# A list scheduler that keeps TensorE on plain fp32 work before it returns to fp32r products

## The chip, the cores and the metric

The kernel runs on one core of a Trainium2 chip. The time is device microseconds of one execution of the whole program on that core, from launch to end; of several runs the median is given. A core has TensorE (PE; its weight loads are a queue of their own, PEld), VectorE (DVE), ScalarE (ACT), GpSimd (POOL) and SyncE (SP), which here only issues DMAs. Each engine works through its own list of instructions in order and waits for the other engines by semaphores.

## The reference

One step of a streaming encoder layer, for a prompt of 512 rows and a sample of 64 rows (576 rows in all, model width 1024). It is all fp32.

```python
h = rms_normalize(x) * g_norm_mix * (1.0 + sc1) + sh1
q, k, v, qi, ki, wi, z, xbc, dt, gate_logits = jnp.split(h @ w_in, offs, axis=-1)
q = rope(rms_normalize(q) * g_q, pos); k = rope(rms_normalize(k) * g_k, pos)
qi = rope(qi, pos); ki = rope(ki, pos)
# branch A: an indexer scores every key, each query keeps the top 128 or 256, softmax over those
logits = jnp.einsum('thd,sd->ths', qi, ki_all); score = sum_h wi * relu(logits)
_, idx = lax.top_k(score, topk); o_attn = softmax(q . k_all[idx]) @ v_all[idx]
# branch B: causal convolution of width 4, Mamba-2 scan in chunks of 64, gated group norm
y, h_last = ssd_scan(silu(causal_conv(xbc)), dt, -exp(a_log), bm, cm, state_ssm)
y = rms_normalize((y + d_skip * xh) * silu(z)) * g_ssm_norm
mixed = (g_attn * (o_attn @ w_branch_attn) + g_ssm * (y @ w_branch_ssm)) @ w_out
x = x + gt1 * mixed
h2 = rms_normalize(x) * g_norm_ffn * (1.0 + sc2) + sh2
gate, up = jnp.split(h2 @ w_gate_up, 2, axis=-1)
x = x + gt2 * ((silu(gate) * up) @ w_down)
```

(Shapes are left out and some lines are drawn together.) Outputs are x of both groups and the new keys, values, indexer keys, convolution rows and SSD states.

## The kernel before

**Three kinds of TensorE work.** Every large product is made of three fp32r products: weights and activations are split into a high part that fp32r holds exactly and a rest (`wh`, `wl`; `hTh`, `hTl` for the activations), and `hTh·wh + hTl·wh + hTh·wl` is summed in PSUM. The split of each weight tile (512 KB, from `raw`) is made by ScalarE (`wh`) and VectorE (`wl`). These are 8,776 of the 10,078 matmuls. What has to be exact, or is small, is plain fp32: 681 transposes against the identity (`ident`) and 94 plain products (the indexer's `kis·qis`, the states' `xw·bt` and others); the profile has two records for each plain product. The third kind, 527 products, are plain fp32 on column tiles: they give `tile_position`, use 32 or 64 columns of the array only, and several of them share it.

**Stages.** Up to about 47 us the modulation vectors and the first norm; to 240 us the projections of q, k, v and of the indexer, and the selection of keys; to 480 us attention over four key heads (`key_stack`, `q_stack`, `softmax_rows`, `pv`, `make_q`), between which `fillers` puts columns of the input projection that are not needed yet (fp32r); to 786 us the convolution and the scan (`conv`, `chunk`, `stage_a`, `stage_b`, `stage_c`), with the rest of the input projection beside it; to 976 us the products of the two branches and of the output; then the feed-forward part, to 1364 us.

**What sets the order.** No instruction is issued where it is written. `Plan` (l.248) records each as an `Op` with its engine, its dependences and a duration from a table (`cost`, l.341). `order` (l.391 to 508) then plays the whole program through by these durations: at each step it takes the engine that is free first, moves what has become ready by then into that engine's heap, and takes the op with the lowest priority number (`op.prio`, the place in which it was written, less an offset that stages give themselves). `emit` (l.511) writes the instructions out in that sequence, so nearly every row of the profile bears the one line 533 (535 with the change), and rows are told apart by the names of their tiles. On the chip each engine keeps the order that the plan found, whatever the real durations are.

**The rule for TensorE** (l.457 to 471). `_columns_of_tile` (l.226) gives an op the width of its column tile, or 0. While the last op taken was on a column tile (`tile_cols` not 0), ops of the same width that are ready go first, even where another has the lower number; and where the width changes, the plan's clock is put forward by 0.095 us. Plain fp32 work and fp32r products both have 0, and between them the priority alone decides. Matmuls of TensorE carry a slack of 0.25 us on their inputs in the plan (`SLACK`).

**Names at the places spoken of.** `tok` are rows from the token-major part that are transposed into `py`/`px` (the PSUM tiles; `mm` is the third pool of PSUM tiles, of the large products). `lg` are the indexer's logits, brought out of PSUM by ScalarE after the products `kis·qis`. In the scan, `ssum`/`sq`·`pick` are column-tile products into `px`, which VectorE copies to `rowsZ`, which TensorE transposes (`px<-ident,rowsZ`); `cu` are steps of the convolution on VectorE (l.1324 on), `xdt` and `xw` scaled inputs of the scan, `xw·bt` the product of the states. `kd` are cached keys, which are transposed for attention.

Of the kernel before, what the change touches and what calls it, by code (L numbers as in the profile page):

```python
# [6 lines left out]
F32R = mybir.dt.float32r  # L7
# [217 lines left out]

def _columns_of_tile(op):

    return op.args[0].shape[0] if op.kw.get("tile_position") is not None else 0


def _cols(v):
# [16 lines left out]
class Plan:  # L248
# [142 lines left out]
    def order(self):  # L391
# [16 lines left out]
        seq, dma_free, queue, now_ev, port, tile_cols = [], 0.0, 0.0, 0, 0.0, 0  # L408

        def enable(op):  # L410
            closed = [p for p in op.pools if not p.open]
            if closed:
                held.setdefault(closed[0], []).append(op)
                return
            t = 0.0
            for d, kind in op.deps.items():
                q = ops[d]
                if q.mm and op.mm:
                    t = max(t, q.t0)
                elif kind == "raw" or q.eng != op.eng:  # L420
                    t = max(t, q.t1 + self.LATENCY[q.eng][op.eng] + op.slack)
            heapq.heappush(future[op.eng], (t, op.prio, op.i))

        def fire():
            nonlocal now_ev
            while now_ev < len(self.events):
                what, p = self.events[now_ev]
                if what == "close" and p.ops_left:
                    return
                seq.append((what, p))  # L430
                now_ev += 1
                if what == "open":
                    p.open = True
                    for op in held.pop(p, []):
                        enable(op)
# [6 lines left out]
        while n < len(ops):  # L442
            best, at = None, None
            for e in engs:
                if ready[e]:
                    t = free[e]
                elif future[e]:
                    t = max(free[e], future[e][0][0])
                else:
                    continue  # L450
                if at is None or t < at:
                    best, at = e, t
            assert best is not None, ("stuck", n, len(ops), self.events[now_ev:now_ev + 1])
            f, r = future[best], ready[best]
            while f and f[0][0] <= at:
                t, pr, i = heapq.heappop(f)
                heapq.heappush(r, (pr, i))
            pr, i = heapq.heappop(r)
            op = ops[i]
            if best == "tensor":  # L460
                if tile_cols and _columns_of_tile(op) != tile_cols:
                    same = [x for x in r if _columns_of_tile(ops[x[1]]) == tile_cols]
                    if same:
                        heapq.heappush(r, (pr, i))
                        pr, i = min(same)
                        r.remove((pr, i))
                        heapq.heapify(r)
                        op = ops[i]
                if _columns_of_tile(op) != tile_cols:
                    at += 0.095  # L470
                tile_cols = _columns_of_tile(op)
            if op.port:
                if port > at and best == "vector":
                    held_back = [(pr, i)]
                    while r and op.port and len(held_back) < 6:
                        pr, i = heapq.heappop(r)
                        held_back.append((pr, i))
                        op = ops[i]
                    pr, i = held_back.pop() if not op.port else held_back.pop(0)
                    op = ops[i]  # L480
                    for x in held_back:
                        heapq.heappush(r, x)
                if op.port:
                    at = max(at, port)
                    port = at + op.dur
            op.t0 = at
            if best == "sync":
                queue = max(at, queue) + 0.46
                dma_free = max(queue + 1.3, dma_free) + op.bytes / 360e3
                op.t1 = dma_free + op.dur_dma  # L490
            elif op.fn == "dma_start":
                dma_free = max(at + op.dur + 1.0, dma_free) + op.bytes / 185e3
                op.t1 = dma_free + op.dur_dma
            else:
                op.t1 = at + op.dur
            free[best] = max(at + op.dur, dma_free - 2.0 if best == "sync" else 0.0)
            seq.append(op)
            n += 1
            for p in op.pools:
                p.ops_left -= 1  # L500
            for s in op.succ:
                ops[s].left -= 1
                if ops[s].left == 0:
                    enable(ops[s])
            fire()
# [35 lines left out]
def build(tc, I, O):  # L541
# [1466 lines left out]
    def prepare_more():  # L2008
        with R.prio(4000):
            more = True  # L2010
            while more:
                more = False
                n = sum(1 for o in slices if o not in rawd and (o in wd or o == ("pair", 0, 0) and ("pair", 0, 1) in wd))
                while loaded[0] < len(slices) and loaded[0] < n + NRAW:
                    load_slice()
                    more = True
                if made[0] < len(order):
                    more = prepare_down() or more
# [106 lines left out]
```

## Time and profile before

| what | value |
|---|---|
| median of 3 runs | 1367.02 us (1366.27 to 1367.84) |
| the profiled execution's own time | 1366.41 us |
| its span, first to last instruction | 1364.4 us |
| mean granted TensorE clock | 0.998 |
| ScalarE busy, whole span | 54% |
| GpSimd busy, whole span | 18% |
| DMA | 199.52 MB, 146 GB/s on average |
| TensorE in the chain that ended last | 89% of the span |

The span is the profiled execution from its first to its last instruction; its own time has 2.0 us more around it. Busy time of TensorE is the union of the matmuls, whose ends are modelled; weight loads (PEld) lie beside them. Rows of the timeline give a start and a duration in us, then the instruction, as output tile, arrow, input tiles; a number behind an x says how many alike follow one another. What stands in brackets is idle time of the engine ahead of the row and what ended it.

### The profile page before, as it was taken

Reading aid. Unit: us, or ns where it says so; the run is one execution under the profiler, and the core shown is the slowest. Engines: PE = TensorE matmul, PEld = TensorE weight load, DVE = VectorE, ACT = ScalarE, POOL = GpSimd, SP = SyncE. Lnnn points to the kernel's source line nnn. Section 1 sums busy time; section 2 is a strip of 40 time slices with the busy share of each in tenths; the row PEclk is TensorE's granted clock in tenths of the full one; section 3 lists DMA queues with packets and bytes.
Section 4 is the critical chain, followed back from the end, with each engine's and each line's share of the span. In section 5 each row is a group of like instructions: output and inputs, shape, how many; then the busy total and the mean of one; then the engine's idle time right before and its main releaser. Section 6 shows DMA issues by size and latency. Waiting matters only on the chain.

```text
span 1364.4 us, 27749 instructions
## 1 busy us (share of the span) xinstructions
PE 1346.8 (99%) x10699; PEld 1311.9 (96%) x10699; DVE 1106.6 (81%) x2237; ACT 733.0 (54%) x1535; POOL 240.2 (18%) x370
## 2 busy tenths in 40 slices
PE   7999999999999999999999999999999999999998
PEld 5999999999999999999999999999999999999998
DVE  5689998887778788888887599857899998878564
ACT  5445343776776766666675342225566665665221
POOL 1312002230310235545453200001000000000000
PEclk9999999999999999999999999999999999999999
DMA  9762435675754454454536698748233343325431
GB/s 298 227 178 84 109 104 140 142 164 126 179 140 116 137 168 118 117 153 122 150 96 193 209 316 241 224 147 257 73 109 94 109 124 94 93 77 156 123 107 36
DMA packets 267332, 199.52 MB, mean 146 GB/s; under 512 B 25152, under 2 KB 239328, under 8 KB 267200
## 3 DMA queue, kind: packets, MB, share of 16 engines
q1 hardware_dynamic: 263248, 183.59, 46.1%
q0 software_dynamic: 3952, 14.16, 5.2%
q8 instruction: 84, 1.38, 0.4%
q14 instruction: 48, 0.39, 0.1%
HBM read 157.75 MB, written 28.96 MB: 137 GB/s over the span
## 4 chain that ended last, share of the span: by engine, by line
PE 89%; DVE 6%; DMA 2%; issue 1%; SPq 1%; ACT 1%; POOL 0%; ACTq 0%; DVEq 0%; POOLq 0%
PE mm L533 64%; PE py L533 14%; PE px L533 11%; DVE score L533 1%; DMA raw<-in_w_in 1%; DVE m L533 1%; DVE wl L533 1%; SPq L533 1%; DMA xt<-in_x_sample 1%; DVE y L533 0%; DVE xlS L533 0%; DMA rawu<-in_w_gate_up 0%; DVE wh L533 0%; DVE tok L533 0%; DVE f L533 0%
## 5 line engine op out<-in xcount | busy, mean ns | idle before, releaser
L533 ACT ACTIVATE wh<-raw 128x1024 fp32r<-128x1024 f32 (+3 forms) x152 | 149.3, 984 | 209.0 <-PE mm L533 149.5
L533 PE MATMUL mm<-hTl,wh 128*128 128x288 f32 (+1 forms) x1024 | 231.9, 302 | 0.0
L533 PE MATMUL mm<-hTh,wh 128*128 128x288 f32 (+1 forms) x1024 | 231.7, 303 | 0.0
L533 PE MATMUL mm<-hTh,wl 128*128 128x288 f32 (+1 forms) x1024 | 230.7, 302 | 0.5 <-DVE wl L533 0.5
L533 PEld LDWEIGHTS mm<-hTh,wh 128*128 128x128 f32 (+1 forms) x1024 | 165.7, 189 | 3.6 <-issue 1.3
L533 PEld LDWEIGHTS mm<-hTl,wh 128*128 128x128 f32 (+1 forms) x1024 | 167.0, 189 | 1.8 <-issue 0.9
L533 PEld LDWEIGHTS mm<-hTh,wl 128*128 128x128 f32 (+1 forms) x1024 | 165.6, 189 | 2.5 <-issue 1.1
L533 DVE TENSOR_TENSOR wl<-raw,wh 128x1024 fp32r<-128x1024 f32 (+2 forms) x109 | 131.3, 1205 | 30.7 <-ACT wh L533 26.3
L533 DVE SCALAR_TENSOR_TENSOR cu<-xc,wc,cu 128x579 f32<-128x579 f32 x96 | 83.4, 869 | 2.0 <-ACT cu L533 1.0
L533 PE MATMUL mm<-wh,hTh 128*128 128x256 f32 x256 | 72.4, 285 | 0.0
L533 PE MATMUL mm<-wh,hTl 128*128 128x256 f32 x256 | 72.2, 284 | 0.0
L533 PE MATMUL mm<-wl,hTh 128*128 128x256 f32 x256 | 71.9, 282 | 0.0
L533 DVE SCALAR_TENSOR_TENSOR aacc<-adr,sil,aacc 128x512 f32<-128x512 f32 x84 | 58.7, 749 | 5.3 <-DMA adr<-in_w_ada 5.2
L533 PE MATMUL mm<-yh,wl 128*128 128x288 f32 x256 | 55.2, 296 | 0.0
L533 PE MATMUL mm<-yh,wh 128*128 128x288 f32 x256 | 55.0, 296 | 0.0
L533 PE MATMUL mm<-yl,wh 128*128 128x288 f32 x256 | 54.9, 296 | 0.0
L533 PE MATMUL mm<-xhS,wh 128*128 128x290 f32 (+1 forms) x248 | 54.8, 296 | 0.0
L533 ACT ACTIVATE P<-lg,mn 128x128 f32<-128x128 f32 (+4 forms) x72 | 41.7, 581 | 19.6 <-DVE mn L533 18.8
L533 PE MATMUL mm<-xhS,wl 128*128 128x290 f32 (+1 forms) x232 | 51.3, 296 | 0.0
L533 ACT ACTIVATE dec<-dec,nacs 128x128 f32<-128x128 f32 x128 | 42.4, 393 | 14.8 <-POOL dec L533 14.8
L533 PEld LDWEIGHTS mm<-wh,hTh 128*128 128x128 f32 x256 | 48.0, 188 | 0.5 <-issue 0.4
L533 PEld LDWEIGHTS mm<-wh,hTl 128*128 128x128 f32 x256 | 48.2, 189 | 0.2
(518 smaller groups left out, 3955.5 us busy)
## 6 DMA issues: line engine op xcount, KB each, us to landing
raw<-in_w_in SPq DMA_DIRECT2D x80, 512.0 KB, 4.3
adr<-in_w_ada SPq DMA_DIRECT2D x36, 512.0 KB, 4.8
raw<-in_w_gate_up SPq DMA_DIRECT2D x22, 512.0 KB, 3.9
wl<-raw POOLq DMA_DIRECT2D x21, 512.0 KB, 5.2
rawu<-in_w_gate_up SPq DMA_DIRECT2D x20, 512.0 KB, 4.0
bc<-acs_d SPq DMA_DIRECT2D x32, 256.0 KB, 3.4
raw<-in_w_branch_ssm SPq DMA_DIRECT2D x16, 512.0 KB, 4.5
raw<-in_w_down SPq DMA_DIRECT2D x16, 448.0 KB, 3.9
```

The costliest lines, as they stand in the source:

```text
L533: getattr(engines[x.eng], x.fn)(*[real(a) for a in x.args], **{k: real(v) for k, v in x.kw.items()})
```

## The change

`_columns_of_tile` now knows three kinds: the width for column tiles, 0 for fp32r products, and -1 for everything else, which is plain fp32 products and all transposes. Since -1 counts as true, the rule "while the last op was of a kind other than 0, ready ops of the same kind go first" now holds for plain fp32 work too: TensorE stays on it while any is ready, and then takes what has the lowest number. From fp32r it leaves as before, as soon as an op of another kind has the lowest number. The second hunk gives a change between plain fp32 and fp32r a price of 0.03 us in the plan; changes to or from a column tile keep 0.095.

```diff
 def _columns_of_tile(op):
 
-    return op.args[0].shape[0] if op.kw.get("tile_position") is not None else 0
+    if op.kw.get("tile_position") is not None:
+        return op.args[0].shape[0]
+    return 0 if op.fn == "matmul" and op.args[2].dtype == F32R else -1
...
                 if _columns_of_tile(op) != tile_cols:
-                    at += 0.095
+                    at += 0.095 if max(_columns_of_tile(op), tile_cols) > 0 else 0.03
                 tile_cols = _columns_of_tile(op)
```

The instructions are the same ones. Their order differs from about 47 us (TensorE's 295th matmul) to 976 us, and behind 790 us only here and there: in 3,762 of TensorE's positions, 642 of VectorE's 2,173, 437 of ScalarE's 1,460, 98 of GpSimd's 375 and 72 of SyncE's 509. Most moves are of a few positions, up to about 50; four transposes of `kd` go from a group at 214 us to 107 us. Groups of plain fp32 work between fp32r products were 263 and are 239; changes between the two kinds were 504 and are 455. The 52 groups on column tiles have the same sizes.

The first place is at about 97 us, TensorE, in the projection of the sample's rows. Before:

```order
L533 MATMUL mm_114<-wl_106,hsS_128 128x256
L533 MATMUL mm_114<-wh_101,hsS_128 128x256
L533 MATMUL mm_114<-wl_104,hsS_128 128x256
L533 MATMUL py_110<-ident_70,tok_651 128x128
L533 MATMUL px_113<-ident_70,tok_651 128x128 x4
L533 MATMUL mm_114<-wh_101,hsS_128 128x256
```

With the change:

```order
L535 MATMUL mm_114<-wl_106,hsS_128 128x256
L535 MATMUL mm_114<-wh_101,hsS_128 128x256
L535 MATMUL py_110<-ident_70,tok_650 128x128
L535 MATMUL px_113<-ident_70,tok_650 128x128 x4
L535 MATMUL mm_114<-wl_104,hsS_128 128x256
L535 MATMUL mm_114<-wh_101,hsS_128 128x256
```

The five transposes of `tok` stand one fp32r product earlier.

The second place is at about 176 us, TensorE, where the indexer's products (`kis·qis`, plain fp32) stand among fp32r products. Before:

```order
L533 MATMUL mm_114<-hTl_127,wh_101 128x288 x2
L533 MATMUL py_110<-kis_670,qis_671 128x384 x2
L533 MATMUL mm_114<-hTh_126,wl_104 128x288 x2
L533 MATMUL mm_114<-hTh_126,wh_101 128x288 x2
L533 MATMUL py_111<-kis_670,qis_671 128x384 x2
```

With the change:

```order
L535 MATMUL mm_114<-hTl_127,wh_101 128x288 x2
L535 MATMUL mm_114<-hTh_126,wl_104 128x288 x2
L535 MATMUL mm_114<-hTh_126,wh_101 128x288 x2
L535 MATMUL py_110<-kis_669,qis_670 128x384 x2
L535 MATMUL mm_114<-hTl_127,wh_101 128x288 x2
L535 MATMUL mm_114<-hTh_126,wl_104 128x288 x2
L535 MATMUL py_111<-kis_669,qis_670 128x384 x2
```

The first index product stands four fp32r products later, the second two.

The third place is at about 568 us, in the scan, behind a group on column tiles. On TensorE, before:

```order
L533 MATMUL px_112<-sq_5063,pick_120 32x64
L533 MATMUL mm_114<-hTh_126,wh_103 128x288 x2
L533 MATMUL mm_114<-hTl_127,wh_103 128x288 x2
L533 MATMUL mm_114<-hTh_126,wl_106 128x288 x2
L533 MATMUL mm_114<-hTh_126,wh_103 128x288 x2
L533 MATMUL mm_114<-hTl_127,wh_103 128x288 x2
L533 MATMUL mm_114<-hTh_126,wl_106 128x288 x2
L533 MATMUL py_111<-xw_5048,bt_5050 128x256
L533 MATMUL mm_114<-hTh_126,wh_103 128x288 x2
L533 MATMUL mm_114<-hTl_127,wh_103 128x288 x2
L533 MATMUL px_113<-ident_70,rowsZ_5034 128x128 x2
```

With the change:

```order
L535 MATMUL px_112<-sq_5040,pick_120 32x64
L535 MATMUL mm_115<-hTh_126,wh_101 128x288
L535 MATMUL mm_115<-hTl_127,wh_101 128x288 x2
L535 MATMUL mm_115<-hTh_126,wl_104 128x288 x2
L535 MATMUL mm_115<-hTh_126,wh_101 128x288
L535 MATMUL py_111<-xw_5025,bt_5027 128x256
L535 MATMUL mm_115<-hTh_126,wh_101 128x288
L535 MATMUL mm_115<-hTl_127,wh_101 128x288 x2
L535 MATMUL px_113<-ident_70,rowsZ_5011 128x128 x2
```

Between the group and the transposes of `rowsZ` stood 16 fp32r products and one plain product, and now stand nine and the same one. On VectorE at that place, before:

```order
L533 TENSOR_TENSOR wl_105<-raw_99,wh_102 128x1024
L533 SCALAR_TENSOR_TENSOR cu_5077<-xc_5075,wc_78,cu_5077 128x579
L533 TENSOR_TENSOR xdt_5046<-px_113,dtp_88 128x256
L533 SCALAR_TENSOR_TENSOR cu_5077<-xc_5075,wc_78,cu_5077 128x579
L533 TENSOR_TENSOR xw_5048<-px_113,wst_90 128x256
L533 SCALAR_TENSOR_TENSOR cu_5077<-xc_5075,wc_78,cu_5077 128x579
L533 COPY rowsZ_5034<-px_112 128x128
```

With the change:

```order
L535 TENSOR_TENSOR xdt_5023<-px_113,dtp_88 128x256
L535 TENSOR_TENSOR xw_5025<-px_113,wst_90 128x256
L535 TENSOR_TENSOR wl_106<-raw_100,wh_103 128x1024
L535 COPY rowsZ_5011<-px_112 128x128
L535 COPY rowsZ_5011<-px_112 32x64
L535 SCALAR_TENSOR_TENSOR cu_5053<-xc_5051,wc_78,cu_5053 128x579
```

The three steps `cu` that stood ahead of the copy and among `xdt` and `xw` stand behind it or elsewhere, and `wl` stands directly ahead of it.

## The prediction

> **What bounds the kernel now.** I began with the page's first two parts, busy time by engine and the 40 slices, to see whether one engine is the limit everywhere.
>
> ```profile
> PE 1346.8 (99%) x10699; PEld 1311.9 (96%) x10699; DVE 1106.6 (81%) x2237; ACT 733.0 (54%) x1535; POOL 240.2 (18%) x370
> PE   7999999999999999999999999999999999999998
> ```
>
> TensorE is busy in 99% of the span and in every slice but the first and the last. A change to its order can therefore gain in two ways only: its instructions take less time in the new order, or its idle time goes. To see where idle time is left I cut the span at the places where the order of the change begins to differ (47 us) and ends to differ (976 us), and once more at 786 us, behind which the two orders are nearly the same.
>
> ```profile
> 0.00:47.00 47.00, 37.73 (x424) 30.18 (x424) 21.82 (x55) 22.55 (x40) 7.32 (x22) 0.96 0.98 294
> 47.00:786.00 739.00, 736.75 (x5919) 714.09 (x5919) 616.09 (x1313) 435.90 (x955) 223.89 (x329) 1.00 0.53 142
> 786.00:976.00 190.00, 190.00 (x1494) 187.45 (x1492) 151.75 (x259) 66.57 (x121) 8.99 (x20) 1.00 0.72 225
> 976.00:1364.40 388.40, 382.33 (x2869) 380.21 (x2867) 316.97 (x612) 207.93 (x420) 0.00 (x0) 1.00 0.34 98
> ```
>
> The second row is the stage that the change reorders (projections, attention, SSD): 739.00 us, of which TensorE is busy in 736.75, so 2.25 us are idle. The idle 15 us of the first and last rows lie where the change moves nothing. Busy PE hides small waits, since the ends of matmuls are modelled. So I also read the waits of the weight loads, which come one ahead of each matmul, in that same stage (waited for, us in total, times, longest).
>
> ```profile
> PEld py L533 <- issue: 4.7, 26, 0.3
> PEld mm L533 <- issue: 2.5, 14, 0.2
> PEld px L533 <- issue: 1.0, 5, 0.3
> PEld py L533 <- DVE tok L533: 1.0, 1, 1.0
> PEld py L533 <- ACT vst L533: 0.9, 1, 0.9
> PEld py L533 <- ACT lg L533: 0.8, 2, 0.6
> PEld px L533 <- POOL dec L533: 0.5, 3, 0.2
> PEld px L533 <- ACT dec L533: 0.5, 3, 0.2
> PEld py L533 <- DVE qst L533: 0.3, 1, 0.3
> PEld px L533 <- DVE qis L533: 0.2, 1, 0.2
> PEld py L533 <- DVE rowsZ L533: 0.2, 1, 0.2
> PEld px L533 <- DVE kst L533: 0.2, 1, 0.2
> ```
>
> The nine rows that name an engine add up to 4.6 us in 14 waits. The three "issue" rows (8.2 us in 45 gaps) wait for nothing that the profile shows; I find them mostly where TensorE goes to or from column tiles. That is all the waiting there is to win in 739 us.
>
> **The change part by part.** It takes no instruction away and adds none: 10,078 matmuls in both orders, and the same work on the other engines. It moves 3,762 positions on TensorE, mostly by fewer than 50. Groups of plain fp32 work between fp32r products fall from 263 to 239, so there are 24 groups fewer; the 52 groups on column tiles keep their number and sizes. The first question is what a group costs beyond its instructions. The timeline of TensorE (start, duration, instruction, count) has a group of one transpose and a group of eight:
>
> ```profile
> 781.74 0.43 PE L533 MATMUL mm<-oh,wh 128*128 128x288 f32 x2
> 782.01 0.29 PE L533 MATMUL mm<-ol,wh 128*128 128x288 f32 x1
> 782.14 0.27 PE L533 MATMUL px<-ident,cvo 128*96 128x128 f32 x1
> 782.17 0.38 PE L533 MATMUL mm<-ol,wh 128*128 128x288 f32 x1
> 782.39 0.42 PE L533 MATMUL mm<-oh,wl 128*128 128x288 f32 x2
> ```
>
> ```profile
> 214.31 0.43 PE L533 MATMUL mm<-hTh,wl 128*128 128x288 f32 x2
> 214.58 1.03 PE L533 MATMUL px<-ident,kd 128*128 128x128 f32 x8
> 215.37 0.51 PE L533 MATMUL mm<-hTh,wh 128*128 128x288 f32 x2
> 215.72 0.43 PE L533 MATMUL mm<-hTl,wh 128*128 128x288 f32 x2
> ```
>
> Starts are to be read here, since durations overlap. Two fp32r products take 0.27 us (781.74 to 782.01), so 0.133 each. From 781.74 to 782.39 is 0.65 us with four of them (0.53), which leaves 0.12 for a group of one transpose. From 214.31 to 215.72 is 1.41 us with four products again, which leaves 0.88 for eight transposes, 0.11 each. If a group cost something to enter or to leave, the one transpose would show all of it: 0.12 less 0.11 is **0.01 us a group**. Terms of the sum:
>
> - 24 groups fewer at 0.01: **-0.24 us**. Bounds: 0, and 0.06 for each (the starts are printed to 0.01 us, and the 0.12 is a difference of several), -1.5 in all.
> - The four transposes of cached keys that go from about 214 us to about 107 us stand amid fp32r products in both places: 0, and their cover is the same work.
>
> The second question is which waits change, since merging moves work past the products that covered its wait. Three places carry the rest. The first is the start of the stage, in the weight loads:
>
> ```profile
> 96.40 0.19 PEld L533 LDWEIGHTS mm<-wl,hsS 128*128 128x128 f32 x1
> 97.57 0.14 PEld L533 LDWEIGHTS py<-ident,tok 128*128 128x128 f32 x1 [0.98 <-DVE tok L533]
> ```
>
> The transposes of tok wait 0.98 us for VectorE. They now stand one product earlier, and a product of 256 columns takes at most the 0.133 us of one with 288; the wait ends when VectorE is done, as before, and the product now runs behind it: **+0.1 us**. Everything behind the transposes on TensorE waits with them. Bounds 0 (if VectorE comes earlier by as much) and +0.13.
>
> The second place is the index product at 175.9 us, which waits for ScalarE's logits to leave PSUM:
>
> ```profile
> 175.16 0.43 PE L533 MATMUL mm<-hTl,wh 128*128 128x288 f32 x2
> 175.92 0.63 PE L533 MATMUL py<-kis,qis 128*128 128x384 f32 x2 [0.33 <-ACT lg L533]
> ```
>
> Two products from 175.16 end at 175.43 by the price above, and the index product starts at 175.92: 0.49 us lost. In the new order four more fp32r products (0.53 us) stand ahead of it and cover all of that: **-0.5 us**. Bounds 0 (ScalarE's evictions, themselves behind an index product, come later by as much) and -0.6, the longest wait of the row "ACT lg". What is late next is the following index product, which keeps its distance of three to four products.
>
> The third place stands for the SSD stage, where three such groups follow a column-tile group:
>
> ```profile
> 567.96 0.43 PE L533 MATMUL mm<-hTh,wl 128*128 128x288 f32 x2
> 568.32 0.45 PE L533 MATMUL px<-ssum,pick 128*32 128x128 f32 x8
> ...
> 568.89 0.28 PE L533 MATMUL px<-sq,pick 128*32 128x64 f32 x2
> 569.10 0.54 PE L533 MATMUL mm<-hTh,wh 128*128 128x288 f32 x2
> ...
> 571.77 0.38 PE L533 MATMUL px<-ident,rowsZ 128*128 128x128 f32 x2
> ```
>
> and VectorE beside it:
>
> ```profile
> 570.32 0.81 DVE L533 SCALAR_TENSOR_TENSOR cu<-xc,wc,cu 128x579 f32<-128x579 f32 x1
> 571.05 0.40 DVE L533 COPY rowsZ<-px 128x128 f32<-128x128 f32 x2
> ```
>
> VectorE's copy of rowsZ ends at 571.45, and its transposes start at 571.77, so 0.32 us are to spare. In the new order seven fp32r products fewer stand ahead of the transposes (7 x 0.133 = 0.93). With the copy as late as before, the transposes would wait 0.93 less 0.32, 0.6 us, at each of three places: +1.8. But VectorE's order changes as well: the convolution steps (cu, 0.81 us each) that stood between ready work and the copy are now two fewer, 1.6 us, which is more than the 0.6. I take **0**, bounds 0 and +1.8, since the new order shows both moves. Before the last wait of attention (ACT vst, 0.9 us) 20 products stand in both orders, so nothing changes there.
>
> The planner also charges 0.03 us at each of 455 switches, which moves other engines' work against TensorE; that is in the order already, and costs nothing by itself.
>
> Sum on the profiled execution (its own time 1366.41, with a span of 1364.4): 1366.41 - 0.24 + 0.1 - 0.5 + 0 = 1365.8. That execution is 0.6 us under the median of the runs (1367.02), so 1366.4 for the median.
>
> **The rivals.**
>
> Faster: merging groups covers most named waits. If all nine rows went, 1366.41 - 0.24 - 4.6 = 1361.6, or 1362.2 for the median. For it: a rule that makes bigger groups leaves longer stretches of fp32r products between them, as at 175.9 us. Against it: of the 4.6 us I find 0.5 that goes; the first two waits (1.9 us) stand behind work that keeps its cover or loses some.
>
> Faster by a price for the switch: entering a column-tile group costs 0.09 us (568.32 less the end of two products from 567.96, 568.23), and leaving about 0.10 (two records of some 0.055 from 568.89 end at 569.00, the next product starts at 569.10). If TensorE paid as much between plain fp32 and fp32r, 24 groups x 0.19 = 4.6 us would go: 1366.41 - 4.6 + 0.1 - 0.5 = 1361.4, or 1362.0. Against it stand the 0.01 us of the single transpose. The Trainium skill's page "TensorEngine Tiling (Array Packing)", section "Key Properties", says that TensorE drains when the tiling mode changes, and not when only the tile does. By that rule a price belongs at the column-tile groups alone, where the trace agrees with 0.19 us; the single transpose at 782.14 shows none.
>
> Slower: merged groups run before their input is ready. A group is prolonged with work that became ready only in the plan; on the chip its producer is late, TensorE works in order, and all fp32r products queued behind it wait too. The price at one place is 0.6 us at worst (rowsZ), and 0.33 us on the mean of the 14 waits (4.6 / 14). It decides the sign from 3.3 us on (2.7 for 0.2%, and the 0.6 gained above): six places at 0.6, or ten at 0.33. If half of the 24 merged groups wait 0.33, it is +4.0: 1369.8, or 1370.4 for the median. For it: the stage has only 2.25 us of idle time, so new waits have no slack to fall into. Against it: groups merge mostly by holding back fp32r products that were ready, and VectorE is busy for 616 of 739 us, ahead of TensorE nearly everywhere.
>
> That the change does nothing is told apart from these by the order: it does merge, though only 24 groups of 263.
>
> **How the numbers follow.** A measurement of this kernel can tell about 0.2% (2.7 us) from no change. The forecast has 0.69; its own range is 1364.9 (all of the -1.5 and -0.6) to 1368.9 (no gain, rowsZ at +1.8 and tok at +0.1). Faster by covered waits gets 0.14, faster by a price of the switch 0.03, slower by late inputs 0.14. The range reaches to 1362.0 and to 1370.4, which leaves out the tails of both sides, and takes in the bounds of each term. Faster 0.17, same 0.69, slower 0.14.
>
> **What would show it.** In the stage 47 to 786 us TensorE's busy time and the length should change by under 2 us. A group of one transpose should still add 0.12 us. The wait for tok should be about 1.1 us, the one for ACT lg at 175.9 us gone, and no wait for rowsZ above 0.2. If groups of equal size take less time than before, the price of the switch is the wrong step. If new rows for VectorE or ScalarE above 0.5 us stand among the waits, it is the cover. A change behind 976 us, where the order is the same, would be no work of this change.

## The result: 0.6% slower, by waits in the attention and scan stages

| | median, us | range | runs |
|---|---|---|---|
| before | 1367.12 | 1366.27 to 1367.84 | 6 |
| with the change | 1375.15 | 1373.79 to 1376.10 | 6 |

The ratio is 1.0058, 95% interval 1.0048 to 1.0069: 8.0 us slower, outside the range that was given (1362.0 to 1370.4). The profiled execution took 1373.79 us, its span 1372.0 us, 7.6 more than before. Of e14, an experiment below, one run is left out of the median: it took 2178.55 us at a granted clock of 0.557.

These are the windows of the changed kernel, cut where the same work begins and ends (us; busy time and count of PE, PEld, DVE, ACT, POOL; clock; DMA share; GB/s):

```profile
0.00:47.00 47.00, 37.23 (x425) 29.71 (x425) 22.12 (x56) 22.80 (x41) 7.64 (x24) 1.00 0.98 295
47.00:794.50 747.50, 740.04 (x5918) 714.60 (x5919) 622.92 (x1312) 435.61 (x955) 233.63 (x327) 1.00 0.52 140
794.50:984.50 190.00, 190.00 (x1493) 187.38 (x1492) 151.79 (x259) 66.62 (x121) 9.00 (x20) 1.00 0.72 225
984.50:1372.00 387.50, 381.98 (x2869) 380.06 (x2868) 316.94 (x612) 208.42 (x420) 0.00 (x0) 1.00 0.34 99
```

The second stage holds all of the loss: 747.5 us for what took 739.0, with as many matmuls (5,918 for 5,919). Up to TensorE's 2,500th record, at 317 us, only 0.4 us of it has come; nearly all of it lies in attention and the scan. The third stage takes the same 190.0, the fourth 0.9 less. TensorE's weight loads are busy for 714.60 us as before (714.09), so TensorE's instructions became no dearer. (The matmuls' busy time is 3.3 us more, but their ends are modelled.) What grew is the waiting of those loads in that stage (engine and line, waited for, us in total, times, longest):

```profile
PEld py L535 <- issue: 4.7, 21, 1.4
PEld py L535 <- ACT decS L535: 3.2, 2, 1.8
PEld mm L535 <- issue: 2.5, 14, 0.2
PEld py L535 <- ACT lg L535: 1.3, 2, 1.1
PEld px L535 <- issue: 0.8, 5, 0.2
PEld py L535 <- ACT qst L535: 0.8, 1, 0.8
PEld px L535 <- DVE dec L535: 0.7, 1, 0.7
PEld py L535 <- DVE qst L535: 0.6, 2, 0.3
PEld px L535 <- DVE xb L535: 0.6, 1, 0.6
PEld py L535 <- DVE tok L535: 0.6, 1, 0.6
...
PEld py L535 <- DVE rowsZ L535: 0.2, 1, 0.2
```

The rows of this view that name an engine or a DMA add up to 13.2 us in 33 waits; before they were 4.6 us in 14. An "issue" row holds a 1.4 us wait that is none of the column tiles' small ones; it is the one at 510 us below. With the three "issue" rows (8.0 us, before 8.2) the view adds up to 21.2 us, before to 12.8. The difference, 8.4 us, accounts for the 8.5 by which the stage is longer.

**Three long waits, all for the states' product xw·bt.** The longest, at 743 us, seen on TensorE, ScalarE, GpSimd and VectorE:

```profile
741.09 0.29 PE L535 MATMUL mm<-hTh,wh 128*128 128x288 f32 x1
743.00 0.67 PE L535 MATMUL py<-xw,bt 128*128 128x256 f32 x2 [1.61 <-DVE xw L535]
```

```profile
740.80 0.35 ACT L535 ACTIVATE decS<-decS,nacs 64x64 f32<-64x64 f32 x1 [1.59 <-POOL decS L535]
741.06 0.85 ACT L535 ACTIVATE cu<-xc,bconv,wc 128x579 f32<-128x579 f32 x1
741.82 0.25 ACT L535 ACTIVATE bt<-px 128x128 f32<-128x128 f32 x1
```

```profile
740.36 0.41 POOL L535 TENSOR_SCALAR_AFFINE_SELECT decS<-bc 64x256 f32<-64x256 f32 x1 [4.70 <-DMA bc<-acs_d]
```

```profile
742.10 0.42 DVE L535 TENSOR_TENSOR xdt<-px,dtp 128x256 f32<-128x256 f32 x1 [2.26 <-ACT bt L535]
742.44 0.41 DVE L535 TENSOR_TENSOR xw<-px,wst 128x256 f32<-128x256 f32 x1
```

Read backwards: TensorE waits for xw, VectorE waits for ScalarE's bt, and bt stands, one convolution step between, behind an exponential of decS that waits for GpSimd, which waits for a DMA. (The waits of the loads above put this wait down to decS at once.) Nothing in bt needs decS; it is only next in line. The same happens at 592.7 us.

That neighbour is not new. Before, all four of these exponentials stood ahead of the same bt, and nothing was lost:

```profile
729.70 1.07 ACT L533 ACTIVATE decS<-decS,nacs 64x64 f32<-64x64 f32 x4 [1.24 <-POOL decS L533]
730.99 0.27 ACT L533 ACTIVATE bt<-px 128x128 f32<-128x128 f32 x1
```

```profile
730.67 0.27 PE L533 MATMUL px<-ident,bcx 128*128 128x128 f32 x1
732.78 0.59 PE L533 MATMUL py<-xw,bt 128*128 128x256 f32 x2
```

There the transpose that bt copies out of PSUM (`px<-ident,bcx`) came 0.97 us behind the first exponential, which therefore held up nothing. In the changed kernel the same transpose is at 739.38, 1.42 us ahead of the exponential. The new order used up what there was to spare between TensorE and the DMA that feeds decS.

At 510.2 us xw·bt waits for its PSUM tile, which VectorE's xb steps free:

```profile
507.90 1.77 DVE L535 SCALAR_TENSOR_TENSOR cu<-xc,wc,cu 128x579 f32<-128x579 f32 x1
509.60 0.46 DVE L535 SCALAR_TENSOR_TENSOR xb<-xb,dcol,py 128x64 f32<-128x64 f32 x2
```

```profile
508.74 0.29 PE L535 MATMUL mm<-hTh,wh 128*128 128x288 f32 x1
510.20 0.67 PE L535 MATMUL py<-xw,bt 128*128 128x256 f32 x2 [1.16 <-DVE xb L535]
```

At 510, 593 and 743 us xw·bt starts 1.46, 1.49 and 1.91 us after the fp32r product ahead of it, which takes 0.13. Lost are 1.33 + 1.36 + 1.78 = 4.5 us, over half of the 8. Before, the same three products started 0.13 us after the one ahead, without a wait.

### The profile page after: what moved, and what is told of

It reads as the page before. It is cut to its first block, busy times and chain, and to the rows that moved or that the text cites. A ratio compares the mean times of both kernels' runs of the same rounds, so it can differ in the third digit from the quotient of the medians.

```text
span 1372.0 us, 27773 instructions
## 1 busy us (share of the span) xinstructions
PE 1349.2 (98%) x10699; PEld 1311.8 (96%) x10699; DVE 1113.8 (81%) x2237; ACT 733.4 (53%) x1535; POOL 250.3 (18%) x370
## 4 chain that ended last, share of the span: by engine, by line
PE 76%; DVE 8%; issue 2%; DMA 2%; ACT 2%; POOL 1%; SPq 0%; ACTq 0%; POOLq 0%; DVEq 0%
PE mm L535 54%; PE py L535 13%; PE px L535 10%; DVE wl L535 1%; DVE score L535 1%; DVE m L535 1%; DVE f L535 1%; DMA bc<-acs_d 1%; DMA o_d<-oT 1%; DVE T L535 1%; DVE cu L535 0%; DVE wh L535 0%; ACT wh L535 0%; DMA rawu<-in_w_gate_up 0%; DVE gg L535 0%
## 5 line engine op out<-in xcount | busy, mean ns | idle before, releaser
L535 DVE SCALAR_TENSOR_TENSOR cu<-xc,wc,cu 128x579 f32<-128x579 f32 x96 | 88.4, 922 | 3.4 <-ACT cu L535 2.2
```

Of the source, the lines that this page charges most:

```text
L535: getattr(engines[x.eng], x.fn)(*[real(a) for a in x.args], **{k: real(v) for k, v in x.kw.items()})
```

## The experiments

All times are medians, beside runs of the kernel before on the same chip (1366.7 to 1367.3). "Waits" is the sum of the rows with a name in the waits of the weight loads, 47 to 795 us; "moved" is how many of TensorE's positions differ from before.

| run | plan | moved | us | ratio, 95% interval | waits, us |
|---|---|---|---|---|---|
| before | | 0 | 1367.1 | | 4.6 |
| change | rule, price 0.03 | 3762 | 1375.2 | 1.0058 (1.0048 to 1.0069) | 13.2 |
| e1 | rule, price 0 | 3035 | 1370.9 | 1.0033 (1.0020 to 1.0046) | 8.6 |
| e2 | no rule, price 0.03 | 3395 | 1379.2 | 1.0094 (1.0072 to 1.0117) | 15.3 |
| e4 | column tiles 0.105 for 0.095 | 2554 | 1378.7 | 1.0084 (1.0069 to 1.0099) | 14.7 |
| e7 | column tiles 0.085 | 2089 | 1370.2 | 1.0024 (1.0015 to 1.0033) | 5.7 |
| e8 | slack 0.26 for 0.25 | 1275 | 1368.1 | 1.0008 (0.9998 to 1.0017) | 7.7 |
| e9 | TensorE's durations x 1.01 | 3965 | 1375.8 | 1.0061 (1.0042 to 1.0080) | 12.8 |
| e10 | TensorE's durations x 0.99 | 4321 | 1378.1 | 1.0078 (1.0061 to 1.0095) | 15.6 |
| e11 | change, durations x 0.99 | 3922 | 1374.6 | 1.0051 (1.0034 to 1.0068) | 9.7 |

**e1 and e2: the rule and the price apart.** The change has two hunks; each was taken alone.

```diff
-                    at += 0.095 if max(_columns_of_tile(op), tile_cols) > 0 else 0.03
+                    at += 0.095 if max(_columns_of_tile(op), tile_cols) > 0 else 0.0
```

> The rule that keeps TensorE on plain fp32 work, with the plan's price of a change between plain fp32 and fp32r at 0 instead of 0.03 us. Same work, 240 groups of plain fp32 work as with the change. If the price does the harm (it makes the plan's TensorE 13.6 us slower over the program than it is, so the plan finds producers on other engines in time that are late on the chip), the time is that of before, 1367 us within 1.5. If the rule does the harm (merged groups stand earlier than their inputs), it is that of the change, 1375 within 1.5. If any reshuffle of this plan does harm, it is somewhere between 1366 and 1376, and its waits stand at other places.

```diff
-                if tile_cols and _columns_of_tile(op) != tile_cols:
+                if tile_cols > 0 and _columns_of_tile(op) != tile_cols:
```

> The price of 0.03 us alone, without the rule: 271 groups of plain fp32 work instead of 240. If the price does the harm, 1375 within 1.5; if the rule does, 1367 within 1.5; if any reshuffle does, between 1366 and 1376.

The loss can't be put down to one hunk. The rule costs 3.7 us without the price (1370.9 less 1367.2), and gains 4.1 with it (1375.2 for 1379.2); the price costs 12 alone and 4.2 beside the rule. e1's longest waits are at places where neither kernel has one: 1.3 us at 377 and 2.0 us at 460, both in attention.

**e4, e7 to e11: controls.** Is it the slower TensorE in the plan (the price puts 13.6 us on it), or any reshuffle? Five of them change one number of the kernel before and have nothing of the rule or its price.

```diff
-                    at += 0.095
+                    at += 0.105
```

(e4; 0.085 in e7.)

> A control: the kernel before with nothing of the change, but 0.105 instead of 0.095 us for a change of column tiles in the plan; 2554 of TensorE's positions differ. If any reshuffle of this plan costs several us, 1369 to 1376; if it takes this rule or this price to do harm, 1367 within 1.5.

> A second control, the kernel before with 0.085 instead of 0.095 us for a change of column tiles in the plan (2089 positions on TensorE differ): the plan's TensorE is faster than it was, not slower. If a plan whose TensorE is too slow does the harm, the time is that of before, 1367.2 within 1.5; if any reshuffle of this plan does, 1369 to 1380, as with 0.105.

```diff
-SLACK = 0.25
+SLACK = 0.26
```

> A third control, the kernel before with a slack of 0.26 instead of 0.25 us on TensorE's inputs in the plan (1275 positions differ): no price is changed, and inputs get more time, not less. If too slow a TensorE in the plan does the harm, 1367.2 within 1.5; if any reshuffle does, 1369 to 1380, with waits at places of its own.

```diff
         op.dur, op.dur_dma = self.cost(op, outs, ins)
+        if eng == "tensor":
+            op.dur *= 1.01
```

(e9; 0.99 in e10, and 0.99 on the changed kernel in e11.)

> The kernel before with all of TensorE's durations in the plan times 1.01, no rule and no price of the change; the plan ends at 1360 us, as late as the change's, because TensorE is planned 13 us slower. If a plan in which TensorE is too slow does the harm, 1375 within 4, as 0.03 us a change alone (1379) and 0.105 us a column tile (1379) gave; if only the luck of a reshuffle counts, as likely 1368 as 1375.

> The same with durations times 0.99: the plan's TensorE is faster than the chip's. If too slow a plan does the harm, 1367 to 1369; if only the luck of a reshuffle counts, it spreads like the others, 1368 to 1379.

> The change with rule and price, and TensorE's durations in the plan times 0.99, so that the plan ends at 1348 us as that of before does and the 13 us that the price put on are taken off again. If too slow a plan does the harm, 1368 to 1371 (the rule alone gave 1370.9); if the price at the places of the changes does it, 1375 within 1.5.

After e4, e7 and e8 it looked as if a too slow TensorE in the plan did it: 0.105 cost 11.5 us, 0.085 cost 3.0 and the slack 0.9. e10 and e11 take that away. A TensorE planned faster than it is costs as much (10.8 us), and the change with its 13 us taken off again stays at 1374.6. What is left is the reshuffle: of nine new plans eight are slower, by 3.0 to 12 us, and e8's 0.9 can't be told from none; those with the most waits are the slowest. e4 shows how little the meaning of a number matters, since its waits are for softmax (P, ptl) and for the convolution's input (xc), neither of which has anything to do with column tiles' prices:

```profile
PEld py L533 <- DVE ptl L533: 3.1, 4, 2.1
PEld mm L533 <- issue: 2.3, 13, 0.2
PEld mm L533 <- ACT xc L533: 2.3, 2, 1.8
PEld px L533 <- DVE P L533: 1.9, 2, 1.7
```

**e3 and e13: the changed order with a few instructions moved.** In e3 the first exponential of decS at 592 and at 743 us goes behind bt, and the step cu at 508 us behind the xb steps:

```diff
         self.seq = seq
+        for late, behind in ((6378, 6178), (8135, 7939), (5287, 5223)):
+            x = ops[late]
+            seq.remove(x)
+            seq.insert(seq.index(ops[behind]) + 1, x)
```

> The changed kernel's order with three instructions moved: at two places ScalarE's first decS exponential (which waits for GpSimd, which waits for a DMA) goes behind the copy bt that stands after it, at one place VectorE's convolution step goes behind the two xb steps that free the PSUM tile. If the three long waits for xw,bt (1.33, 1.35 and 1.78 us in the profile) are lost time that these three places make, the time falls by 4.2 us, to 1371 within 1; if they only show lateness that comes back at the next wait, it falls by less than 1.5.

Measured: 1372.31 us, 1.0034 (1.0024 to 1.0045), 2.8 us less than the change, about two thirds of the 4.2 and between the two forecasts. (The eight runs spread from 1369.8 to 1373.8, and the change was not run again beside them.) The three waits are gone, and the longest that are left in the view are others:

```profile
PEld py L539 <- ACT lg L539: 1.3, 2, 1.1
PEld px L539 <- issue: 1.2, 6, 0.3
PEld py L539 <- ACT qst L539: 0.8, 1, 0.8
```

From TensorE's 2,500th to its 6,000th record, the stretch that holds the three, the profiled executions take 429.5 us before, 437.1 with the change and 432.1 with the moves. TensorE's order is the same in the last two, and 1.33, 1.35 and 1.78 us come back exactly at the three products. Another 1.1 us comes back at 479 and 484 us, ahead of the moved instructions: e3's profiled execution was 2 us later than the change's from 57 us on, which can cover waits there. So the mechanism is shown for these three places (4.5 us of the profiled execution, 2.8 of the median): an instruction on a feeding engine that stands behind one it doesn't need costs TensorE over 1 us at a time, once nothing is left to spare.

e13 adds seven more moves on VectorE, at the next longest waits:

```diff
+        for moved, behind in (
+                (6378, 6178), (8135, 7939), (5287, 5223), (576, 881), (577, 576), (1103, 1092), (1107, 1103),
+                (2269, 2265), (4920, 4986), (4977, 4921)):
```

> The changed order with the three moves of e3 and seven more on VectorE, at the next longest waits of TensorE (tok at 97 us, the index product at 177, attention's first product at 246, the first two transposes of the scan at 479 and 484; 3.3 us in all). If the rest of the loss is waits of this kind, and half to all of each is kept, 1369 to 1371; if it is something else, 1372.3 as with e3.

Measured: 1372.31 us, 1.0041 (1.0027 to 1.0054), no better than e3; its waits are 10.3 us, and e3's 8.6. The wait for the index product went from 1.04 us at 177 to 1.62 us at 181, a few products later. There the moves passed the wait on, and what makes the rest of the loss was not taken back by any run.

**e5 and e6: merge and split by hand.** Here the order of before is kept on every other engine, and only fp32r products change places with groups of plain fp32 work.

```diff
+        if r < len(pe) and r - e <= 4 and plain(pe[r]) and all(bring(x, first) for x in pe[e:r]):
+            pe[k:r] = pe[e:r] + pe[k:e]
```

(`pe[k:e]` is a group, `pe[e:r]` the products between it and the next; `bring` puts a product ahead of `first`, the group's first instruction, where its inputs stand earlier.)

> The kernel before with groups of plain fp32 work merged by hand and nothing else moved: up to four fp32r products between two groups go ahead of the first, where their inputs stand earlier in the program; 190 groups instead of 264, 299 of TensorE's positions differ, every other engine's order is that of before. If a change between plain fp32 and fp32r costs 0.01 us a group, 74 groups fewer give 0.7 us less, within what can't be measured: 1366.5 within 1. If it costs what the change charges (0.03 us at each of 148 changes fewer), 4.4 us less: 1362.8. If merged groups meet late inputs by themselves, 1370 or more.

Measured: 1370.96 us, 1.0029 (1.0019 to 1.0039), with waits of 10.2 us. Merging by itself costs, with nothing else moved. One of its places, on TensorE:

```profile
691.63 0.43 PE L571 MATMUL mm<-hTh,wh 128*128 128x288 f32 x2
691.90 0.38 PE L571 MATMUL px<-bcx 128*128 128x128 f32 x2
692.44 0.67 PE L571 MATMUL py<-xw,bt 128*128 128x256 f32 x2 [0.15 <-DVE xw L571]
```

Four fp32r products stood between these two in the order of before. Now xw·bt follows bcx directly, 0.54 us after a product that takes 0.22, so 0.32 us are lost. Before, the product behind those four lost 0.19 there; three such places make 0.4 us more. Three groups of transposes of r, in the same stage, wait 0.32 to 0.36 us each for GpSimd, where they waited for nothing before.

```diff
+            for x in pe[e:r]:
+                if at < e and bring(x, pe[at]):
+                    new += [x, pe[at]]
+                    at += 1
```

> The opposite by hand: fp32r products that follow a group of plain fp32 work go in between its transposes; 602 groups instead of 264, all other engines in the order of before. At 0.01 us a group the time is 1367.2 + 3.4 = 1370.5; at 0.03 us for each of 676 changes more it is 1387; at nothing 1367.

Measured: 1376.12 us, 1.0058 (1.0041 to 1.0075). Its timeline measures the price of a group directly, since eight transposes now stand singly between products:

```profile
217.36 0.43 PE L578 MATMUL mm<-hTh,wl 128*128 128x288 f32 x2
217.63 0.27 PE L578 MATMUL px<-ident,kd 128*128 128x128 f32 x1
217.65 0.38 PE L578 MATMUL mm<-hTh,wh 128*128 128x288 f32 x1
...
219.35 0.27 PE L578 MATMUL px<-ident,kd 128*128 128x128 f32 x1
219.37 0.38 PE L578 MATMUL mm<-hTh,wh 128*128 128x288 f32 x1
219.59 0.43 PE L578 MATMUL mm<-hTl,wh 128*128 128x288 f32 x2
```

From 217.36 to 219.59 are 2.23 us for ten products (1.33) and eight transposes (0.88), 2.21 in all: 0.02 us for eight groups, some 3 ns each. So 338 groups more cost about 1 us of the 8.9, and the waits rose by 4.9 (9.5 for 4.6). About 3 us stay open. (The profiled execution was 2.4 us later than before's at 57 us, but no instruction ahead of that had been moved.) The expectation that read 3.4 us at 0.01 a group had the price too high and left the waits out.

**e15 and e16: whose order is it?** TensorE's order of one kernel was joined with that of the other engines of the other kernel. Where the two would block each other, the next instruction that can go is taken.

```diff
-        self.order()
+        self.both_orders(True, False)
...
+        queues = {e: list(lists[tensor_from if e == "tensor" else others_from][e]) for e in lists[True]}
```

> TensorE in the order of the change, all other engines in that of before (131 instructions stand out of place, where the two orders would block each other). If TensorE's order carries the loss, 1375 within 2; if the others' does, 1367 within 2; if what counts is that the orders fit each other to a few tenths of a us, more than either, above 1377.

> The reverse: TensorE in the order of before, all other engines in that of the change (116 instructions out of place). If TensorE's order carries the loss, 1367 within 2; if the others' does, 1375 within 2; if the fit of the orders counts, above 1377.

(The lines are e15's; e16 has the two the other way round.) Measured: 1519.3 us (1.1095, 1.1068 to 1.1121) and 1504.1 us (1.1004, 1.0989 to 1.1019). Both are far slower than either kernel, though nearly all moves of the change are local. The waits of e15, the first two rows:

```profile
PEld py L603 <- ACT pth L603: 26.7, 13, 4.1
PEld px L603 <- DVE dec L603: 26.6, 13, 3.6
```

So one engine's order can't be exchanged alone; it has to fit the others'. Whose order carries the 8 us these two runs don't tell. How much of the 137 to 153 us the instructions out of place make (131 and 116) was not taken apart. A part may be the clock: between 400 and 600 us of e15 TensorE is busy for 154 of 200 us, and the granted clock is 0.86.

**e12 and e14: the same moves in the kernel before.** Against its waits at 97.6, 175.9 and 247.2 us:

```diff
+        for moved, behind in ((576, 881), (577, 576), (1103, 1032), (2282, 2267)):
```

> The kernel before with three small moves on VectorE alone, against its three longest waits between 47 and 786 us: the two aacc steps go behind the qi1 step that the transposes of tok wait for (0.93 us lost in the profile), the first score step goes ahead of wl (0.49), a qst step goes two places forward (0.90). If such waits are lost time, 1367.2 - 2.3 = 1364.9 within 0.7; if they come back at the next wait, 1367.2 within 0.7.

Measured: 1366.12 us, 0.9991 (0.9983 to 1.0000), about half of what was hoped. The wait at 97.6 us is gone; the one at 247.2 us shrank from 0.90 to 0.79 us. The index product at 175.9 now starts at once, and the next one waits, 0.67 us beyond the products ahead of it:

```profile
176.02 0.51 PE L539 MATMUL py<-kis,qis 128*128 128x384 f32 x2
...
176.63 0.42 PE L539 MATMUL mm<-hTh,wh 128*128 128x288 f32 x2
177.57 0.62 PE L539 MATMUL py<-kis,qis 128*128 128x384 f32 x2 [0.51 <-ACT lg L539]
```

e14 moves those two as well:

```diff
-        for moved, behind in ((576, 881), (577, 576), (1103, 1032), (2282, 2267)):
+        for moved, behind in ((576, 881), (577, 576), (1103, 1032), (1107, 1103), (2282, 2267), (2280, 2285)):
```

> The kernel before with six moves on VectorE: those of e12, and the two instructions at which its second and third wait came back (0.68 and 0.79 us there) moved as well. If waits between 47 and 250 us are lost time, 1367.2 - 2.2 = 1365.0 within 0.7; if they come back once more, 1366.1 as with e12.

Measured: 1367.37 us, 1.0003 (0.9994 to 1.0012). The waits are 4.2 us in place of 5.4, and no time is won that can be told. No order that beats the kernel before clearly was found.

## Why the prediction was wrong

**What bounds the kernel** was read rightly: TensorE, with the stage from 47 us to the end of the scan as the place that the change reorders. All of the loss is there.

**The price of a group** was small as forecast: for transposes 3 ns by e6, where I had put 0.01 us. 24 groups fewer give 0.07 us instead of 0.24. The rival that a change of kind drains TensorE for 0.19 us is out, and so is the plan's own 0.03.

**"Three places carry the rest"** is the step that failed. I compared the products ahead of three waits that the trace of before had, and took every other place to keep its cover. That put every wait which the new order makes at nothing. It has 33 waits with a name where there were 14, and the two largest kinds (xw·bt, 4.5 us; the start of the scan at 479 to 486 us, some 1.4 us) are at instructions that waited little or not at all before. A list of the waits of before shows what is late now; it has no row for what has little to spare, and that is what a reshuffle uses up. By the sign that the prediction named for it (new rows above 0.5 us for VectorE or ScalarE) it was the cover, and the stage changed by 8.5 us where under 2 was forecast.

**The three places themselves.** For tok I gave +0.1; its wait went from 1.0 to 0.6 us, because VectorE's steps ahead of it, which wait for a DMA, began 0.45 us earlier in that execution. For rowsZ I gave 0, and 0.2 us is what there is. For the index product I gave -0.5, as four products more would cover its wait:

```profile
174.94 0.40 DVE L533 TENSOR_SCALAR score<-lg,wi 128x384 f32<-128x384 f32 x1
```

```profile
175.92 0.41 DVE L535 TENSOR_SCALAR score<-lg,wi 128x384 f32<-128x384 f32 x1
```

```profile
175.60 0.43 PE L535 MATMUL mm<-hTh,wh 128*128 128x288 f32 x2
176.91 0.62 PE L535 MATMUL py<-kis,qis 128*128 128x384 f32 x2 [0.88 <-ACT lg L535]
```

The score step that frees lg starts at 175.92, 0.98 us later than before (174.94, the L533 row); VectorE's order changed too. The wait became 1.04 us where it had been 0.49. I had named that case ("come later by as much") and taken it as the bound, not as the value.

**The rival that came nearest** is the slower one, merged groups that run before their input is ready, for which I gave 0.14 and 4.0 us (twelve waits at 0.33). Late inputs were right, and e5 shows that merging can make them, with all other engines unchanged: +3.7 us. But merging isn't needed for it: e2 merges nothing and loses 12 us with 15.3 us of waits. Its size was not right either: there are 19 waits more, and the mean is 0.40 (13.2 / 33). What I held against it, that VectorE is "ahead of TensorE nearly everywhere", was read from VectorE's busy time; 623 of 747 us busy leaves much idle, but says nothing of whether one instruction of it comes in time. And its place was too narrow: the long waits come from ScalarE's and VectorE's orders, which the prediction followed at rowsZ alone.

**What I didn't have as a rival** is that nearly any new plan is slower. Nine plans other than that of before, five of them with numbers that have no meaning for this change, took 1368 to 1379 us. The loss of 8.0 us is in the midst of these, and the rule itself, 3.7 us without the price and -4.1 with it, has no sign of its own. Why the plan of before is better than all its neighbours stays open: the runs show that it has fewer waits, not why.

## What to carry to other kernels

Where a planner decides the order and the bounding engine has no idle time, judge a change of its rules by the spread of meaningless changes to it (a slack or a price by 0.01 us, durations by 1%) before giving the rule credit or blame; here that spread was 0.9 to 11.5 us, and the saving in the switches themselves 0.07. Before you group instructions to save a switch, measure the switch in a row of alternating ones. In reading an order, look less at who is busy than at what stands directly ahead of each small copy that the bounding engine needs, and at how much time there is to spare there.

## What the runs showed of the hardware that was not expected

A single 128x128 transpose in fp32 between fp32r products costs TensorE some 3 ns beyond its own 0.11 us (eight in 0.02 us, e6), against 0.19 us for a group on column tiles.

VectorE's convolution step at 507.90 us, which makes the wait at 510 us, took 1.77 us; the median of the 96 like it is 0.82. GpSimd was in a large step when it began:

```profile
507.78 1.28 POOL L535 TENSOR_TENSOR cs<-bc,bcx 128x512 f32<-128x512 f32 x1
```

That step ends at 509.06; 0.81 us from there would be 509.87, and VectorE's step ended at 509.67. The Trainium skill's page "SBUF — State Buffer", section "SBUF: two separate sides", says that a VectorE instruction with two inputs in SBUF and a GpSimd instruction that reads SBUF lock each other out for a whole instruction. The trace agrees to 0.2 us: five more of these steps, at 471, 564, 572, 714 and 722 us, took 1.72 to 1.87 us, and all six end 0.61 to 0.62 us behind a GpSimd step that was running when they began. No run here took GpSimd's step away to show it. Such steps alone don't make a plan slow: e7 has ten above 1.3 us, the change six, and e7 loses 3.0 us. In the stage of the loss VectorE is busy for 622.92 us (616.09 before) and GpSimd for 233.63 (223.89) with the same work; no run shows how much of that is such overlap.
